# Splitting half of the scan's operator evictions between VectorE and ScalarE, with a new order of the scan's stages and of the end, in a bidirectional RWKV-7 layer

## The chip, the cores and the metric

The kernel runs on one core of a Trainium2 chip. The metric is the device time of one execution in microseconds; the time of before is the median of three runs. A core has TensorE (PE; its weight loads are listed as PEld), VectorE (DVE), ScalarE (ACT), GpSimd (POOL) and SyncE (SP, which issues the DMAs here). Each works through its own list of instructions in order; they meet at semaphores.

## The reference

The layer mixes 128 context tokens and 2048 latent tokens of width 1024. Half of the width goes through RWKV-7 heads (8 of 64 channels), in both directions; the other half is a short gated convolution. What matters here is the recurrence of a head:

```python
def step(S, inp):                    # S: 64x64 state of each head and direction
    r_t, w_t, k_t, v_t, kk_t, a_t = inp
    s_kk = jnp.einsum('bdhij,bdhj->bdhi', S, kk_t)
    S = (S * w_t[..., None, :] - s_kk[..., :, None] * (kk_t * a_t)[..., None, :]
         + v_t[..., :, None] * k_t[..., None, :])
    return S, jnp.einsum('bdhij,bdhj->bdhi', S, r_t)
s_final, ys = lax.scan(step, s0, xs)
y = ys[:, 0] + jnp.flip(ys[:, 1], axis=1)     # then a norm per head, a bonus term, a gate
...
u = concat([ya, yb]) @ w_out
return x + gate * u, s_final                  # and a final RMS norm of x
```

The context starts from zero states and returns its final ones; the latent tokens start from cached states.

## The kernel before

Phase 1 (to about 950 us) makes the projections, the convolution and the scan's inputs. Phase 2 is the scan, phase 3 the output projection with the final norm.

**The scan in stages.** A sequential recurrence is turned into matmuls over chunks of 64 tokens. There are 17 stages, 0 to 16; stage 15 is the context. A stage takes, for each direction (0 and 1), eight units; a unit is one chunk of a pair of heads. Its work is cut into words, and the last digit of a word is the direction:

- `L` loads the inputs of a direction (`rr`), `fs`, `gs` and `sv` further ones (tiles `stf`, `stg`/`sth`, `sv`); all are DMAs of SP.
- `Gm`, `Qm`, `Fm` are products on PE into PSUM; `Ge`, `Fe` (DVE, with a mask, L1037) and `Qe`, `Fa` (ACT, copies) bring them to SBUF. `F` is split so: ACT copies columns 0 to 63, DVE masks columns 64 to 127.
- `dg`, `ab` (DVE, L1058 and L1063) gather 32x32 blocks, `zi` (ACT) writes an identity, `pre` (DVE, L1081 and L1082) multiplies and subtracts once, and `I` inverts the blocks on POOL: 45 instructions a stage, 15 multiplications (L1091) and 30 subtractions (L1094). `I` waits for `pre` of its stage.
- `zr`, `zd` (DVE transposes, L1102 and L1105), `c0`, `c1` (ACT), `U` (PE), `bu` (ACT), `W` (PE), `n` (ACT, L1130) join the blocks to 64x64 inverses, in this order. `X` solves on PE; `Xc` (ACT, L1175) copies the result to `stf`.
- `E` makes the operators: eight words a stage, `Eijd` with d the direction, each 16 matmuls (L1189) into one PSUM tile of 128x512; `Ev` brings it to SBUF on DVE with a mask (L1194).
- `S` (PE, L1220) and `sv` (DVE, L1246) are the recurrence itself: eight state steps a direction, each of which needs the `sv` before it. `y` collects outputs; for the context `sv` writes `so`, which goes to DRAM as a final state.
- `fw`, `fr`, `fq`, `fm`, `T`, `fy`, `fa` finish a block of outputs.

**The order.** The string SEQ is one body: the words in the order in which each engine gets them, where `X+k` is word X of stage b+k in body b. PE, DVE and ACT keep this order in bodies 0 to 12 (FIXED = 13); ahead of these a scheduler places the words, and it places POOL's and SP's instructions everywhere. From body 13 to the end the string LATE is the order, where `X@s` is word X of stage s. It also holds phase 3's words: `WL`, `WH`, `WD` load and split the output weight (`woh`, `wol`), `AL`, `AH`, `AD` and `CL`, `CH`, `CD` load and split the inputs (`mhc`, `mlc`), `AP0@t`, `AP1@t` are the twelve matmuls each (tile `psa`) of the convolution's half of the inputs of token tile t with either half of the output's columns, which need no output of the scan, and `R`, `Lo` change pools.

**PSUM.** IN_PM lists the words whose tiles come from the pool `pm`; `T`, `U`, `W` and `S` share `pS`, the rest `p2`. A product in PSUM waits for a free buffer of its pool, which comes back when its eviction is done.

Of the kernel before, what the change touches and what calls it, by code (L numbers as in the profile page):

```python
# [10 lines left out]
ALU = mybir.AluOpType  # L11
# [741 lines left out]


SEQ = """
S00 sv51+-1 fa+-1 S61+-1 Ge0+3 dg0+3 gh10+1 sv61+-1 E110 sv00 S71+-1 svL1+1 y10+-1 Ev001 S10 c1+1 Ev110 sv10
E111 sv71+-1 Ev111 E010 E101 y11+-1 E011 gsL1+2 fsL1+1 bu+1 Ev010 I+2 S20 Ev101 fw Ev011 sv20 S01 E100
fsL0+1 gsL0+2 sv01 fr Ev100 Gm1+3 Ge1+3 dg1+3 W+1 S11 Qm1+3 gh11+1 gh00+1 ab+3 fq Fm0+3 S30 n+1 Qe1+3 Qm0+3
L0+4 sv11 Fa0+3 Qe0+3 zi+3 sv30 S40 Fe0+3 fm S21 sv40 sv21 Fm1+3 L1+4 X0+1 S50 pre+3 T sv50 Fa1+3 Fe1+3 S31
S60 sv31 Xc00+1 init+1 y00 Xc10+1 X1+1 S41 Xc01+1 sv60 S70 svL0+2 zr+2 sv41 E000+1 sv70 fy Xc11+1 Ev000+1  # L760
zd+2 S51 gh01+2 U+2 y01 Gm0+4 E001+1 c0+2
"""
IN_PM = "E001 E011 E101 E110 Fm1 Gm1 Qm0 Qm1 X1".split()
IN_S = "T U W".split()
FIXED = 13
LATE = """
I@15 sv51@12 fa@10.1 Ge0@16 E110@13 Ev001@13 gh10@14 E010@13 Ev110@13 E100@13 gh00@14 Ev010@13 Gm1@16
fsL0@14 Ev100@13 gh11@14 S00@13 Ge1@16 S61@12 E111@13 c1@14 sv00@13 E011@13 sv61@12 bu@14 dg0@16 S10@13
Ev011@13 S71@12 E101@13 svL1@14 fw@11.0 sv10@13 sv71@12 y10@12 S20@13 fsL1@14 Ev111@13 S01@13 y11@12 W@14
sv20@13 sv01@13 Ev101@13 S30@13 n@14 S11@13 sv30@13 sv11@13 S40@13 fr@11.0 X0@14 sv40@13 fq@11.0 dg1@16  # L770
X1@14 fm@11.0 Xc00@14 ab@16 S50@13 S21@13 Xc10@14 T@11.0 Xc01@14 E000@14 sv50@13 sv21@13 S60@13 Ev000@14
E010@14 zi@16 Xc11@14 sv60@13 S31@13 Ev010@14 S70@13 E100@14 svL0@15 sv70@13 sv31@13 pre@16 I@16 E110@14 Ev100@14
fy@11.0 E001@14 fsL0@15 gsL0@15 gh00@15 Ev110@14 S00@14 Fm1@16 gh10@15 sv00@14 fa@11.0 S10@14 E011@14
fw@11.1 Fa1@16 y01@13 sv10@14 y10@13 Ev011@14 S41@13 S20@14 y00@13 sv41@13 E111@14 sv20@14 Ev001@14
S51@13 S30@14 sv51@13 E101@14 sv30@14 zr@15 S61@13 fsL1@15 gsL1@15 gh01@15 S40@14 sv40@14 U@15 sv61@13 zd@15
gh11@15 S50@14 fr@11.1 S71@13 svL1@15 c0@15 sv50@14 sv71@13 S60@14 Ev111@14 c1@15 sv60@14 Ev101@14 S70@14
svL0@16 sv70@14 Fm0@16 bu@15 Fe1@16 y10@14 Qm1@16 Fa0@16 S01@14 fq@11.1 W@15 sv01@14 Qe1@16 Fe0@16 S11@14
fm@11.1 n@15 Qm0@16 sv11@14 Qe0@16 X0@15 R@0 CL@5 CL@4 S21@14 Xc00@15 T@11.1 sv21@14 S31@14 fy@11.1 Xc10@15
sv31@14 fa@11.1 y11@13 X1@15 y00@14 S41@14 Xc01@15 sv41@14 y01@14 S51@14 Xc11@15 sv51@14 S61@14 sv61@14
S71@14 CH@4 E110@15 svL1@16 sv71@14 E100@15 CH@5 CD@4 fw@14.0 CD@5 WL@0 zr@16 WL@1 zd@16 U@16 fr@14.0 c1@16  # L780
y11@14 c0@16 Ev100@15 Ev110@15 E111@15 bu@16 E101@15 Ev111@15 WH@0 E000@15 Ev101@15 WH@1 E001@15 WD@0
Ev000@15 fq@14.0 E011@15 fm@14.0 W@16 fsL1@16 gsL1@16 gh01@16 Ev001@15 WD@1 CL@7 Ev011@15 E010@15 gh11@16
T@14.0 fsL0@16 gsL0@16 gh10@16 S00@15 CL@6 fy@14.0 S30@15 S20@15 S01@15 gh00@16 S11@15 fa@14.0 S31@15 S21@15
sv30@15 n@16 Ev010@15 sv00@15 sv20@15 fw@14.1 X1@16 CH@7 fr@14.1 S10@15 S40@15 S60@15 Xc01@16 CD@7 S70@15
Xc11@16 sv40@15 WL@3 sv11@15 sv01@15 sv21@15 sv10@15 CH@6 X0@16 S50@15 CD@6 Xc00@16 S41@15 S61@15 S51@15
sv51@15 Xc10@16 WL@2 sv50@15 sv41@15 sv70@15 sv31@15 fq@14.1 E110@16 fm@14.1 E000@16 sv60@15 WH@3 sv61@15
S71@15 Ev110@16 sv71@15 E111@16 WD@3 Ev000@16 E001@16 Ev111@16 E101@16 Ev001@16 WH@2 AL@5 E100@16 y10@15
WD@2 Ev100@16 y00@15 T@14.1 E010@16 fy@14.1 S00@16 fa@14.1 S01@16 Ev010@16 AH@5 E011@16 AD@5 AL@6 Lo@0 xL@5
sv00@16 AP0@5 y01@15 y11@15 aL@5 fc@15.1 AP1@5 AE0@5 Ev101@16 fw@15.1 fr@15.1 xL@6 sv01@16 Ev011@16 AH@6
S10@16 S11@16 AE1@5 AD@6 aH@5 sv10@16 AP0@6 AL@7 fq@15.1 aD@5 fm@15.1 aL@6 sv11@16 AP1@6 AE0@6 P0l@5 B0@5  # L790
AH@7 AE1@6 AD@7 aH@6 cL@8 aD@6 aL@7 AP0@7 Z0@5 G0@5 AP1@7 AE0@7 P1l@5 B1@5 AE1@7 cH@8 cD@8 cL@9 P0l@6 B0@6
# [24 lines left out]
def phase2(K):
    nc, tc, A, S = K.nc, K.tc, K.A, K.S
    V, G, P, T = nc.vector, nc.gpsimd, nc.scalar, nc.tensor
    D = nc.sync.dma_start
    MF, MG, ME = (0, 1), (0, 1), (2, 3)  # L820
    B = Ctx()
# [151 lines left out]
    def stage(s):  # L973

        if s in sts:
            return sts[s]
        st = sts[s] = Ctx()
        st.g = []
        st.fin = None
        for d, units, blk in stages[s]:  # L980
            g = Ctx()
            g.d, g.units, g.blk = d, units, blk
            g.E, g.ps, g.sp = {}, {}, {}
            st.g.append(g)
        return st

# [190 lines left out]
    def operator(name, s, st, gi):  # L1177

        g = st.g[gi]
        n, h2 = (int(c) for c in name[-3:-1])  # L1180
        us = half(g, n)
        k = (h2 if g.d == 0 else 1 - h2) * 2
        if name[:2] != "Ev":
            lt, rt = (g.fs, g.gs) if g.d == 0 else (g.gs, g.fs)
            pe = g.ps[name] = psum(name, s, [128, 2, 2, 128])
            for i in range(2):
                for hd in range(2):
                    for b, r in enumerate((H0, H1)):
                        T.matmul(pe[r, i, hd, :].rearrange("p (b t) -> p b t", b=2), lt[:, b, hd, us.start + k + i], rt[:, :, hd, us.start + k + i], start=True, stop=True)  # L1189
# [4 lines left out]
        V.tensor_tensor(g.E[n][:, k:k + 2].rearrange("p a b c -> p (a b) c"), pe[:].rearrange("p a b c -> p (a b) c"),  # L1194
                        B.msk[:, ME[g.d]].unsqueeze(1).broadcast_to((128, 4, 128)), ALU.mult)
# [137 lines left out]
    def ending(name, s, st, gi):  # L1333
# [3 lines left out]
        if st.fin is not None:  # L1337
# [311 lines left out]
```

## Time and profile before

| | us |
|---|---|
| median of 3 runs | 1579.01 (1577.63 to 1589.78) |
| profiled execution | 1579.98 |
| its span, first to last instruction | 1578.2 |
| busy: PE, DVE, ACT, POOL | 1496.3, 1138.5, 772.6, 574.6 |
| granted TensorE clock, mean | 0.989 |
| inverses of stages 2 to 16 on POOL, first start to last end | 963.21 to 1331.81 |

The shares of busy time are averages over three phases; the page's row of POOL in 40 slices stands at 8 tenths in the scan and at 0 to 3 elsewhere. The answers used below are of five kinds: the waits of an engine (total, times, longest), its timeline (start, length, engine, line, operation, out<-in, shape, how many instructions are joined; in brackets the idle time before, and who ended it), groups by line and shape (how many, then busy time and mean ns, then idle time before), busy time by window, and transfers by tile.

### The profile page before, as it was taken

The numbers are of one execution on the slowest core, as the hardware profiler recorded it, in microseconds if no ns is written. First come the engines' busy times: TensorE is split into PE (matmuls) and PEld (weight loads), VectorE is DVE, ScalarE is ACT, GpSimd is POOL, SyncE is SP. The second block draws the span as 40 slices with busy tenths as digits, with TensorE's granted clock in tenths as the row PEclk, the third lists the DMA queues.
The fourth block names the chain that finished last, engine by engine and source line by source line (L and its number), as shares of the span: only waits on it lengthen the run. The fifth ranks groups of instructions, "written<-read, shape, count | busy, mean of one in ns | idle before, by whom it ended". The sixth has DMA issues, their size and how long they took to land.

```text
span 1578.2 us, 39386 instructions
## 1 busy us (share of the span) xinstructions
PE 1496.3 (95%) x16208; PEld 1377.9 (87%) x16208; DVE 1138.5 (72%) x1957; ACT 772.6 (49%) x1462; POOL 574.6 (36%) x962
## 2 busy tenths in 40 slices
PE   5899989999999999999999998999999997799998
PEld 2899989999999999899999997887888786678786
DVE  5999995673999735449995437899898987646533
ACT  4566652432555313225651107887878777523222
POOL 0133320000333100013322805888888887212221
PEclk9999999999999999999999998999999999999999
DMA  9669998663877875447887536566675754645442
GB/s 370 211 186 264 265 266 324 214 217 118 214 228 228 200 241 182 142 140 205 257 252 267 196 124 170 163 185 174 192 202 163 192 157 149 183 139 189 149 143 93
DMA packets 204580, 313.78 MB, mean 199 GB/s; under 512 B 58089, under 2 KB 147561, under 8 KB 190321
## 3 DMA queue, kind: packets, MB, share of 16 engines
q1 hardware_dynamic: 168816, 311.13, 63.6%
q10 hardware_dynamic: 35584, 0.14, 1.4%
q8 instruction: 127, 2.08, 0.6%
q14 instruction: 53, 0.43, 0.1%
HBM read 208.05 MB, written 103.17 MB: 197 GB/s over the span
## 4 chain that ended last, share of the span: by engine, by line
PE 61%; DVE 18%; DMA 8%; issue 5%; POOL 4%; ACT 3%; SPq 1%; ACTq 0%; DVEq 0%; POOLq 0%
PE psu L1503 4%; PE psu L1504 4%; PE psu L1505 4%; PE psE L1189 3%; POOL zt L1094 3%; PE mmb L182 2%; PE mmb L184 2%; PE mmb L183 2%; PE psS L1220 2%; PE mmc L182 2%; PE mmc L184 2%; PE mmc L183 2%; PE mmu L184 2%; PE mmgb L184 2%; PE mmu L182 2%
## 5 line engine op out<-in xcount | busy, mean ns | idle before, releaser
L1094 POOL TENSOR_TENSOR zt<-zt,ztmp 128x30 f32<-128x30 f32 (+7 forms) x510 | 217.6, 427 | 39.8
L1091 POOL TENSOR_TENSOR ztmp<-ab,zt 128x60 f32<-128x60 f32 (+7 forms) x255 | 138.2, 542 | 63.7 <-DVE ab L1082 44.0
L410 POOL TENSOR_TENSOR sh<-rawl 128x384 f32<-128x384 f32 (+1 forms) x48 | 46.9, 994 | 209.9 <-ACT rawl L401 209.9
L1220 PEld LDWEIGHTS psS<-sv,E 128*64 128x64 f32 x2176 | 81.3, 138 | 40.3 <-DVE sv L1246 18.8
L1220 PE MATMUL psS<-sv,E 128*64 128x64 f32 x2176 | 102.2, 229 | 14.8 <-DVE sv L1246 11.0
L1194 DVE TENSOR_TENSOR E<-psE,msk 128x512 f32<-128x512 f32 x136 | 90.6, 683 | 16.6 <-PE psE L1189 15.4
L1568 POOL TENSOR_TENSOR z<-z,x 128x512 f32<-128x512 f32 x32 | 42.7, 1338 | 146.5 <-DVE z L1562 86.0
L1175 ACT ACTIVATE stf<-psX 64x512 f32<-64x512 f32 x136 | 80.3, 591 | 11.2 <-PE psX L1171 8.8
L434 POOL TENSOR_TENSOR hsl<-sq,hsh 128x384 fp32r<-128x384 f32 (+1 forms) x24 | 34.0, 1417 | 130.6 <-ACT hsh L429 130.6
L1246 DVE TENSOR_TENSOR sv<-psS,pc 64x128 f32<-64x128 f32 x254 | 62.7, 273 | 22.5 <-PE psS L1220 21.8
L182 PE MATMUL mmg<-h,w 128*128 128x384 f32 (+1 forms) x216 | 70.8, 328 | 0.0
L183 PE MATMUL mmg<-h,w 128*128 128x384 f32 (+1 forms) x216 | 70.7, 327 | 0.0
L184 PE MATMUL mmg<-h,w 128*128 128x384 f32 (+1 forms) x216 | 70.6, 327 | 0.0
L219 POOL TENSOR_TENSOR hslq<-ssq,hshq 128x384 fp32r<-128x384 f32 (+1 forms) x4 | 4.8, 1208 | 176.9 <-ACT hshq L218 176.9
L182 PE MATMUL mmb<-h,w 128*128 128x384 f32 (+1 forms) x192 | 63.6, 331 | 5.8 <-DMA w<-scr_wsp 3.3
L184 PE MATMUL mmc<-h,w 128*128 128x384 f32 (+1 forms) x192 | 63.5, 331 | 0.9 <-DVE w L154 0.9
L182 PE MATMUL mmv<-h,w 128*128 128x384 f32 (+1 forms) x192 | 63.0, 328 | 1.0 <-DVE sg L524 0.9
L182 PE MATMUL mmc<-h,w 128*128 128x384 f32 (+1 forms) x192 | 63.6, 331 | 0.0
L184 PE MATMUL mmb<-h,w 128*128 128x384 f32 (+1 forms) x192 | 63.5, 331 | 0.0
L183 PE MATMUL mmc<-h,w 128*128 128x384 f32 (+1 forms) x192 | 63.3, 330 | 0.0
L183 PE MATMUL mmb<-h,w 128*128 128x384 f32 (+1 forms) x192 | 63.3, 330 | 0.0
L184 PE MATMUL mmu<-h,w 128*128 128x384 f32 (+1 forms) x192 | 62.8, 327 | 0.0
(312 smaller groups left out, 5009.8 us busy)
## 6 DMA issues: line engine op xcount, KB each, us to landing
w<-scr_wsp SPq DMA_DIRECT2D x68, 1024.0 KB, 6.8
scr_wsp<-w SPq DMA_DIRECT2D x34, 1024.0 KB, 6.1
rr<-scr_ops SPq DMA_DIRECT2D x32, 1024.0 KB, 6.2
scr_ops<-xs SPq DMA_DIRECT2D x160, 192.0 KB, 6.1
wr<-in_win SPq DMA_DIRECT2D x34, 512.0 KB, 6.8
x<-in_x SPq DMA_DIRECT2D x17, 512.0 KB, 3.7
wadas<-in_wada SPq DMA_DIRECT2D x8, 1024.0 KB, 13.7
sv<-scr_vt SPq DMA_DIRECT2D x32, 256.0 KB, 3.8
```

Of the source, the lines that this page charges most:

```text
L182: T.matmul(ps[:, :n], w[:, 0, k], hh[:, 0, k, :n], start=k == 0, stop=False)
L183: T.matmul(ps[:, :n], w[:, 0, k], hh[:, 1, k, :n], start=False, stop=False)
L184: T.matmul(ps[:, :n], w[:, 1, k], hh[:, 0, k, :n], start=False, stop=k == 7)
L1091: G.tensor_tensor(tv, ab[:, j:j + 2, j + 2:32].unsqueeze(1).broadcast_to((128, kn, 2, n)), zt[:, :kn, j:j + 2].unsqueeze(3).broadcast_to(( ...
L1094: G.tensor_tensor(zt[:, :kn, j + 2:32], zt[:, :kn, j + 2:32], tv[:, :, r], ALU.subtract)
L1175: P.activation(g.fs[64:128, :, hd, e::2], g.ps["X"][e][hr_].rearrange("p a (b t) -> p b a t", b=2), AF.Copy, scale=-1.0)
L1194: V.tensor_tensor(g.E[n][:, k:k + 2].rearrange("p a b c -> p (a b) c"), pe[:].rearrange("p a b c -> p (a b) c"), B.msk[:, ME[g.d]].unsquee ...
L1220: T.matmul(g.sp[i // 4][r, q, hd, :], g.E[n][:, k, hd, r], g.sv[:, u, hd, :], start=True, stop=True)
L1246: V.tensor_tensor(dst, g.sp[i // 4][0:64, q], B.pc[0:64, d, 2 * p:2 * p + 2, c:c + 1].broadcast_to((64, 2, 64)), ALU.mult)
L1503: T.matmul(ps[:], mh[:, n], hi[:, cs], start=start and n == 0, stop=False)
L1504: T.matmul(ps[:], mh[:, n], lo[:, cs], start=False, stop=False)
L1505: T.matmul(ps[:], ml[:, n], hi[:, cs], start=False, stop=stop and n == 3)
```

## The change

A new word `Ea` lets ACT copy columns 0 to 63 of an operator, for four of the eight words of a stage (E000, E001, E100, E101). No mask applies to these columns. `Ev` of such a word then covers columns 64 to 127 alone; it follows `Ea` in the list and waits for it. All three order strings are new.

```diff
+        dst, pe = (x.rearrange("p a b c -> p (a b) c") for x in (g.E[n][:, k:k + 2], g.ps["E" + name[-3:]][:]))
+        if name[:2] == "Ea":
+            P.copy(dst[:, :, 0:64], pe[:, :, 0:64])
+            g.plain.add(name[-3:])
+            return
+        c0 = 64 if name[-3:] in g.plain else 0
+        V.tensor_tensor(dst[:, :, c0:], pe[:, :, c0:], B.msk[:, ME[g.d], c0:].unsqueeze(1).broadcast_to((128, 4, 128 - c0)), ALU.mult)
+        g.ps.pop("E" + name[-3:])
...
-IN_PM = "E001 E011 E101 E110 Fm1 Gm1 Qm0 Qm1 X1".split()
+IN_PM = "E011 Fm0 Fm1 Gm0 Gm1 X1".split()
...
-fsL0+1 gsL0+2 sv01 fr Ev100 Gm1+3 Ge1+3 dg1+3 W+1 S11 Qm1+3 gh11+1 gh00+1 ab+3 fq Fm0+3 S30 n+1 Qe1+3 Qm0+3
+fq U+1 Qm0+3 Qe1+3 sv20 S21 Ge1+3 dg1+3 ab+3 fm S30 sv21 Fm0+3 E110 L0+4 gh00+1 Ev110 bu+1 W+1
```

In SEQ the loads are spread: `L0+4` stands at 0.48 of the list and `L1+4` at 0.77 (0.54 and 0.66 before), the `fs` loads at 0.60 and 0.64 (0.35 and 0.25), the `gs` loads at 0.59 and 0.89 (0.24 and 0.36). The first operator of the next stage stands 0.27 of the list behind its `fs` load, `Gm0+4` 0.51 behind `L0+4`. `U` of a stage moves from the end of one body to 0.36 of the next. In LATE, `Gm` to `pre` of stage 16 come near the beginning, and `AP0@5`, `AP1@5`, `AP0@6` stand between the words of stages 15 and 16.

Below, the first number behind `psF`, `psX` or `psE` is the stage, the two behind `psS` are the direction and the first step of a half (0 or 4), the rest number buffers; shapes are partitions x elements. Lines of `phase2` have moved by one, and from the operators on by six (L1194 is now L1200, L1246 is L1252, L1306 is L1312).

The first place is DVE in a full body (stage 6's operators, stage 9's products), from `ab` to the first instruction of `pre`. Before:

```order
L1063 STREAM_TRANSPOSE ab_13008<-dg_12786 128x32x32
L1246 TENSOR_TENSOR sv_12319<-psS_1_0_12921,pc 64x128
L1246 TENSOR_TENSOR sv_12194<-psS_0_0_12772,pc 64x128
L1037 TENSOR_TENSOR F_8365<-psFm_9_1356_13011,msk 128x4x64
L1037 TENSOR_TENSOR F_8365<-psFm_9_1357_13012,msk 128x4x64
L1305 RECIPROCAL yss_12938<-yss_12938 128x8
L1306 TENSOR_TENSOR y_10261<-y_10261,yss_12938 128x512
L1246 TENSOR_TENSOR sv_12194<-psS_0_4_13051,pc 64x128
L1246 TENSOR_TENSOR sv_12319<-psS_1_0_12921,pc 64x128
L1081 TENSOR_TENSOR dg_12786<-ab_13008 128x512
```

Now:

```order
L1064 STREAM_TRANSPOSE ab_12985<-dg_12884 128x32x32
L1311 RECIPROCAL yss_12898<-yss_12898 128x8
L1312 TENSOR_TENSOR y_10363<-y_10363,yss_12898 128x512
L1252 TENSOR_TENSOR sv_12315<-psS_1_0_12878,pc 64x128
L1200 TENSOR_TENSOR E_1339_12807<-psE_6_1357_13014,msk 128x512
L1038 TENSOR_TENSOR F_8365<-psFm_9_1355_12996,msk 128x4x64
L1038 TENSOR_TENSOR F_8365<-psFm_9_1356_12997,msk 128x4x64
L1252 TENSOR_TENSOR sv_12254<-psS_0_0_12764,pc 64x128
L1200 TENSOR_TENSOR E_1346_12896<-psE_6_1360_13074,msk 128x512
L1082 TENSOR_TENSOR dg_12884<-ab_12985 128x512
```

Two whole operator evictions have moved in between `ab` and `pre`, and two of the four state steps there have moved out.

The second place is ACT in the same body, from the last copies of a solve to the merge of the stage after it. Now:

```order
L1176 ACTIVATE stf_9577<-psX_6_1325_12667 64x2x4x64 x2
L1196 COPY E_1330_12735<-psE_6_1329_12726 128x4x64
L1273 COPY y_12771<-psS_1_0_12388 64x512
L1161 COPY stg_9583<-GA_8369 64x8x64
L1162 COPY stg_9583<-Q_8370 64x8x64
L1112 COPY zb<-zd_12695 32x16x32 x2
L1196 COPY E_1337_12799<-psE_6_1336_12786 128x4x64
L1196 COPY E_1339_12807<-psE_6_1335_12775 128x4x64
L1273 COPY y_12771<-psS_1_4_12697 64x512
L1273 COPY y_12646<-psS_0_4_12650 64x512
```

The rows of L1196 are new, here three of the stage's four; the others were there before, in another order.

The third place is PE near the end, at stage 16's solve and operators. Before, from the last rows of the operators on:

```order
L1317 MATMUL psT_1743_17473<-idt_8359,y_16671 128x2x64 x4
L1189 MATMUL psE_16_1744_17478<-stg_9582,stf_9576 64x128 x8
L1220 MATMUL psS_0_0_17489<-sv_16807,E_1736_17430 64x64 x4
L1220 MATMUL psS_1_0_17497<-sv_17018,E_1740_17452 64x64 x4
L1189 MATMUL psE_16_1745_17506<-stf_9577,stg_9583 64x128 x8
L1503 MATMUL psa_0_17536<-woh_16928,mhc_17503 128x512
```

Now, from the end of the solve to the first operators and the third product:

```order
L1172 MATMUL psX_16_1727_17444<-F_8374,zb 64x128 x2
L1226 MATMUL psS_0_4_17282<-sv_16761,E_1710_17218 64x64 x4
L1226 MATMUL psS_0_4_17282<-sv_16761,E_1702_17136 64x64 x4
L1226 MATMUL psS_1_4_17477<-sv_16724,E_1705_17176 64x64 x8
L1226 MATMUL psS_1_4_17477<-sv_16724,E_1707_17196 64x64 x8
L1190 MATMUL psE_16_1734_17512<-stf_9577,stg_9583 64x128 x8
L1190 MATMUL psE_16_1735_17525<-stg_9582,stf_9576 64x128 x8
L1509 MATMUL psa_0_17540<-woh_16707,mhc_17440 128x512
```

The first matmul of `psa` stood behind the last operator; now one `psa` group stands ahead of each half of the solve, one behind the first two operators, and state steps of stage 15 (`psS_0_4`, `psS_1_4`) lie ahead of these.

More of the change, by code (lines that the diff above doesn't have):

```diff
@@ L772 @@
[L772 to L791, printed above, removed]
@@ new lines @@
+S21@15 AP1@5 Xc10@16 fa@14.0 sv21@15 y01@15 sv70@15 AH@6 X1@16 AD@6 S60@15 Xc01@16 S50@15 WL@3 sv60@15
+S41@15 S51@15 sv50@15 S71@15 sv41@15 S61@15 sv51@15 Xc11@16 sv71@15 sv61@15 y10@15 E001@16 WH@2 y11@15
+E100@16 fc@15.1 Ea001@16 WD@2 AP0@6 Ea100@16 AE1@5 Ev001@16 Ev100@16 WH@3 AL@7 E111@16 AE0@6 WD@3 fw@15.1
+E010@16 Ev111@16 E110@16 Ev010@16 E000@16 Ev110@16 fr@15.1 E101@16 Ea000@16 Ev000@16 Ea101@16 E011@16
+fq@15.1 Ev101@16 AP1@6 Lo@0 Ev011@16 aL@5 xL@5 fm@15.1 AH@7 S01@16 T@15.1 sv01@16 AE1@6 AD@7 S11@16 S00@16
@@ new lines @@
+sv11@16 AP0@7 cL@8 sv00@16 xL@6 aH@5 fy@15.1 aD@5 fa@15.1 aL@6 AP1@7 AE0@7 P0l@5 S21@16 AE1@7 B0@5 sv21@16
+cH@8 aH@6 cD@8 aD@6 aL@7 cL@9 S31@16 S10@16 sv31@16 P1l@5 B1@5 y01@16 sv10@16 Z0@5 G0@5 S41@16 aH@7 S20@16
+sv41@16 P0r@6 B0@6 sv20@16 aD@7 Q0@5 Z1@5 aL@8 G1@5 S51@16 S30@16 sv51@16 P1r@6 sv30@16 S61@16 y00@16 S40@16
+xL@7 Q1@5 B1@6 sv61@16 sv40@16 Z0@6 ss@5 G0@6 aH@8 S71@16 S50@16 sv71@16 P0l@7 rt@5 B0@7 y11@16 sv50@16
+fw@16.1 aD@8 Q0@6 fr@16.1 aL@9 Z1@6 fq@16.1 S60@16 P1l@7 B1@7 sv60@16 G1@6 fm@16.1 rc@5 fo@5 xL@8 S70@16
```

82 lines of the change are left out of this document (45 added, 37 removed).

## The prediction

> **What bounds the kernel now.** I read the window table first, because the span mixes three phases. Its columns are window, length, then busy time and instruction count of PE, PEld, DVE, ACT and POOL, then the granted clock.
>
> ```profile
> 963.21:1331.81 368.60, 341.54 (x8756) 300.07 (x8750) 322.25 (x654) 291.93 (x552) 315.98 (x684) 1.00 0.63 175
> 1125.00:1149.50 24.50, 23.08 (x597) 20.17 (x593) 24.01 (x50) 18.51 (x36) 21.05 (x45) 1.00 0.70 198
> 1331.80:1372.30 40.50, 29.88 (x601) 25.80 (x597) 27.36 (x51) 24.23 (x38) 12.18 (x6) 0.94 0.56 164
> 1372.30:1389.00 16.70, 15.52 (x80) 11.85 (x78) 7.72 (x15) 4.67 (x10) 0.10 (x1) 1.00 0.75 236
> 1389.00:1570.60 181.60, 181.60 (x864) 145.62 (x862) 89.19 (x148) 48.09 (x118) 42.73 (x32) 1.00 0.44 142
> ```
>
> The first row holds 15 inverses of the scan, the second one stage out of it, where DVE is busy 24.01 of 24.50 us. By that row DVE looks like the bound, and the change takes work from DVE. The waits of POOL say otherwise:
>
> ```profile
> POOL ztmp L1091 <- DVE ab L1082: 14.5, 1, 14.5
> ```
>
> This is every wait that POOL has in 963 to 1331.8 us (total, times, longest), and it is the one with which the window begins. The timeline of POOL shows a seam between two inverses:
>
> ```profile
> 963.21 0.29 POOL L1091 TENSOR_TENSOR ztmp<-ab,zt 128x60 f32<-128x60 f32 x1 [14.51 <-DVE ab L1082]
> ...
> 1157.68 0.60 POOL L1094 TENSOR_TENSOR zt<-zt,ztmp 128x30 f32<-128x30 f32 x2
> 1158.36 0.29 POOL L1091 TENSOR_TENSOR ztmp<-ab,zt 128x60 f32<-128x60 f32 x1
> ...
> 1307.15 0.63 POOL L1215 MEMSET sv<- 64x128 f32 x4
> ...
> 1331.21 0.60 POOL L1094 TENSOR_TENSOR zt<-zt,ztmp 128x30 f32<-128x30 f32 x2
> ```
>
> An inverse ends at 1158.28, the next begins at 1158.36. From 963.21 to 1331.81 they follow each other so: 368.60/15 = 24.57 us each. POOL's busy sum (315.98) hides this, since it leaves out the short pauses between its 684 instructions. Who follows whom is seen on DVE:
>
> ```profile
> 1155.51 0.69 DVE L1082 TENSOR_TENSOR ab<-ab,dg 128x512 f32<-128x512 f32 x1
> 1158.31 1.08 DVE L1102 STREAM_TRANSPOSE zr<-zt 128x512 f32<-128x512 f32 x1
> 1182.74 1.08 DVE L1102 STREAM_TRANSPOSE zr<-zt 128x512 f32<-128x512 f32 x1 [1.32 <-POOL zt L1094]
> ```
>
> DVE ends the preparation (`pre`) of the next inverse at 1156.20, 2.16 us before POOL takes it up, and starts `zr` at 1158.31, 0.03 us after the inverse's end; for the next `zr`, at 1182.74, it idles 1.32 us. So **POOL bounds the scan** and DVE keeps 2 to 3 us in hand. From 1331.81 PE bounds: in the last window it is busy for 181.60 of 181.60 us, and ahead of that it idles 40.50 − 29.88 + 16.70 − 15.52 = **11.8 us**. Only these 11.8 us, the seams and the start can be won without a faster POOL.
>
> **The change, part by part.**
>
> *The split eviction.* The two engines' prices are in the window's groups:
>
> ```profile
> L1194 DVE TENSOR_TENSOR E<-psE,msk 128x512 f32<-128x512 f32 x120 | 79.9, 683 | 12.0 <-PE psE L1189 10.9
> L1037 DVE TENSOR_TENSOR F<-psFm,msk 128x256 f32<-128x256 f32 x58 | 21.5, 411 | 0.7 <-ACT F L1051 0.7
> L1051 ACT COPY F<-psFm 128x256 f32<-128x256 f32 x58 | 18.9, 376 | 9.8 <-PE psFm L1019 9.8
> ```
>
> Eight evictions (120/15) belong to a stage. Four of them go from 128x512 (683 ns) to 128x256, and `F` is that size: 4 × (683 − 411) = 1.09 us less on DVE a stage; four copies like `F`'s come to ACT, 4 × 376 = 1.50 us. ACT goes from 18.5 to 20 of 24.5 us. Value on the path: **0**, since POOL covers both; if POOL were no cover it would be −1.1 us a stage (a rival below).
>
> Does it lengthen or shorten POOL's inverse? DVE work stretches POOL's instructions only in some cases. POOL's timeline beside DVE's:
>
> ```profile
> 1129.99 1.40 POOL L1091 TENSOR_TENSOR ztmp<-ab,zt 128x112 f32<-128x112 f32 x1
> 1134.63 0.38 POOL L1091 TENSOR_TENSOR ztmp<-ab,zt 128x112 f32<-128x112 f32 x1
> 1130.01 1.11 DVE L1081 TENSOR_TENSOR dg<-ab 128x512 f32<-128x512 f32 x1
> ...
> 1145.05 0.99 POOL L1094 TENSOR_TENSOR zt<-zt,ztmp 128x128 f32<-128x128 f32 x2
> 1120.29 0.99 POOL L1094 TENSOR_TENSOR zt<-zt,ztmp 128x128 f32<-128x128 f32 x2
> 1144.71 1.89 DVE L1194 TENSOR_TENSOR E<-psE,msk 128x512 f32<-128x512 f32 x3
> ```
>
> The same multiplication takes 1.40 us under `pre` and 0.38 without it; the pair of subtractions takes 0.99 under three operator evictions and 0.99 elsewhere. Halving these evictions gives POOL **0**.
>
> The two halves of an operator lie in one PSUM tile, as those of `F` do, and there DVE waits for ACT:
>
> ```profile
> DVE F L1037 <- ACT F L1051: 0.7, 1, 0.7
> ```
>
> So a split operator is ready 376 + 411 = 787 ns after its product at the earliest, against 683 now, and DVE, which works in order, stands at its half until ACT has come to the copy. [...]
>
> *The start* (the first inverse of the steady part begins at 963.21). Both `Gm` products of stage 2 now share one PSUM pool; PE still has its transposes and products of other stages around them. Bounds −0.4 and +0.5, taken **+0.1**.
>
> *The first ordered body.* There the preparation is just in time:
>
> ```profile
> 981.61 2.13 DVE L1063 STREAM_TRANSPOSE ab<-dg 128x1024 f32<-128x1024 f32 x1
> ...
> 986.30 0.69 DVE L1082 TENSOR_TENSOR ab<-ab,dg 128x512 f32<-128x512 f32 x1
> ```
>
> It ends at 987.00 and the inverse before it at 987.12. The new list puts two full evictions between `ab` and `pre`: 2 × 0.68 − 0.12 = 1.25 us late if `ab` stays where it is, 0 if the work taken out ahead of `ab` moves it up, and 2 if the evictions wait for PE as well. I take **+1.0**. In later bodies the same two evictions eat 1.4 of the 2.2 us in hand, while 1.1 us comes back from the smaller ones: **0**.
>
> *The moved loads.* SP's transfers, from issue to landing:
>
> ```profile
> rr<-scr_ops SPq DMA_DIRECT2D x25, 1024.0 KB, 5.6
> stf<-scr_ops SPq DMA_DIRECT2D x28, 256.0 KB, 5.0
> ```
>
> The closest user after the move is the first operator of a direction-0 stage, 0.27 of the list behind its `fs` load, 6.6 of 24.6 us against 5.0; `Gm` stands 0.5 of the list, 12 us, behind its `L`, against 5.6. They stay hidden: **0**. If `fs` landed 3 us later, 1.4 us of wait would begin on PE, inside the 2 to 3 us in hand.
>
> *The last seam.* Four small memsets of the context's states (from 1307.15) delay the last inverse, which starts at 1307.76; four more and a copy of a held state (0.28) interrupt it later. In the new order `pre` of stage 16 comes early, and POOL has all eight memsets inside the last inverse and the copy behind it. The memsets cost their 1.26 us there as before: **−0.3** (−0.6 if they find POOL idle, +0.5 if one waits for its buffer).
>
> *The end.* PE's largest idle times after the last inverse:
>
> ```profile
> PE psE L1189 <- DVE E L1194: 6.4, 5, 3.8
> PE psX L1171 <- ACT stf L1175: 1.4, 2, 0.8
> PE psU L1119 <- DVE zr L1102: 1.0, 1, 1.0
> ...
> 1362.94 0.28 DVE L1246 TENSOR_TENSOR so<-psS,pc 64x128 f32<-64x128 f32 x1 [3.96 <-DMA out_nst<-so]
> 1372.27 0.50 PE L1503 MATMUL psa<-woh,mhc 128*128 128x512 f32 x1
> 1377.66 0.39 PE L1505 MATMUL psa<-woh,mlc 128*128 128x512 f32 x1
> 1388.53 0.50 PE L1503 MATMUL psa<-woh,mhc 128*128 128x512 f32 x1 [1.18 <-ACT mhc L1490]
> ```
>
> The longest, 3.8 us, is an operator's product that waits for an eviction, which stands on DVE behind `so`, and that waits for the transfer of an earlier state. The new list gives PE work for such times: AP0@5 and AP1@5 are the 24 matmuls from 1372.27 to 1378.05, 5.8 us or 2.9 each, and with AP0@6 8.7 us are placed between stage 16's merges, solves and operators. It also leaves more of PE's work behind the last inverse: two operators of stage 15 (0.9) and four state steps of stage 14 (4 × 0.46), 2.8 us. Without any idle, therefore, the end gains 11.8 − 2.8 = 9.0; with all of it left, it loses 2.8. I walked the new order after the last inverse by these durations. Before, stage 16's operators end 40.5 us after it, and with the 8.7 of AP and the 1.2 of idle at 1388.53 this is 50.4. In the new order the same work is 29.9 + 2.8 + 8.7 = 41.4, and I find 3.5 us of idle (the merge `U` waits for `zr`, `W` for the copies of the merge, and one solve for its copies), since products that need no scan stand next to each longer wait: 44.9. Value **−5.5**. What is late next is the chain `zr`, `U`, `W`, `X` itself, and from 1389 on PE's own work.
>
> The sum goes against the profiled execution, 1579.98 us (1.8 beside its span), 0.97 above the median of the runs, 1579.01: 1579.98 + 0.1 + 1.0 − 0.3 − 5.5 = **1575.3**.
>
> **The rivals.**
>
> *The end stays as it is.* The new fillers need `mhc` tiles from ACT, whose list at the end gets stage 16's copies too; if these are late, PE waits at AP instead. Then 1579.98 + 0.1 + 1.0 − 0.3 = 1580.8, and up to 2.8 more: about 1582. For it: the wait for `mhc` at 1388.53. Against it: at 40.5 us ACT is busy for 24.2 only. It is inside the range.
>
> *DVE bounds the full stages.* Then 1.1 us comes off each of the 13 ordered bodies, and the sum is 1575.3 − 14.2 = 1561. For it: 24.01 of 24.50. Against it: DVE's idle before `zr`, and POOL's lack of any wait.
>
> *Slower: DVE waits for ACT.* DVE's half eviction has `ab` and `pre` behind it, and ACT has its copy behind others that wait in their turn:
>
> ```profile
> ACT zb L1130 <- PE psW L1127: 21.4, 15, 4.6
> ```
>
> That is 1.4 us a stage. If each of the four copies finds ACT held up that long, DVE stands 4 × 1.4 = 5.7 us at its halves; it has 2.6 us in hand and 1.1 from the smaller evictions, so 2.0 a body reach POOL: 13 × 2.0 = 26, about 1601. It decides from 3.7/4 = 0.93 us a copy; at half the delay nothing is seen. For it: the wait is new, and sits ahead of `pre`. Against it: in ACT's new order the copies stand behind those of `stf`, `zb` and `y`, and none directly behind the wait for `W`.
>
> *The change does not do as it says*: the operators come later than before, so that state steps wait though DVE is freed. That is the mechanism just named at a smaller size, 0 to +10: 1575 to 1585.
>
> **How the numbers follow.** Forecast with its bounds, 0.70: the low end is 1579.98 − 0.4 + 0 − 0.6 − 9.0 = 1570, the high end 1579.98 + 0.5 + 2.0 + 0.5 + 2.8 = 1586; it takes in the rival with the unchanged end. DVE as the bound: 0.11. Slower by DVE's waits for ACT: 0.13. Late operators past 1586: 0.06. The range goes from **1566 to 1588**; below it remains most of DVE as bound (about 0.09), above it most of the slower rival (0.11). One per cent, 15.8 us, is about what a measurement of this kernel can tell from no change. Faster by more, under 1563.2: 0.09. Slower by more, over 1594.8: 0.09. Within: 0.82.
>
> **What the profile after would show.** POOL's inverses follow each other with 0.08 us from about 963 on, with one seam near 987 of up to 2 us; an inverse still takes 24.6 us. If DVE waits for ACT, its row of waits for `E` from ACT is over 3.7 us a stage, and POOL has a wait for `ab` L1083 in many bodies. On DVE the evictions fall into two groups of 64, and ACT has 68 copies of `E` near 376 ns. After the last inverse PE's idle up to the steady end is about 6 us instead of 11.8, the first `psa` stands before stage 16's solve, and no wait of 3.8 us remains on PE for `E`. The prediction is wrong if POOL waits for `pre` in the ordered bodies, if an inverse's own time changes from 24.6 us, or if the last window is not full on PE.

## The result: slower by 0.8 per cent, and the profile after

The changed kernel takes 1596.60 us (median of 20 runs) against 1582.04 for the one before (20 runs): a ratio of 1.0083, 95% interval 1.007 to 1.0096. The forecast was 1575.3, with a range that ended at 1588. The profiled execution took 1594.97 us, its span 1593.0, 14.8 more than the span before.

First the waits of POOL, again from the start of the steady scan to the last inverse (total, times, longest):

```profile
POOL ztmp L1092 <- DVE ab L1083: 44.7, 10, 15.2
```

Before, there was one wait, of 14.5 us, with which the window began. Now there are nine more, 29.5 us in all. POOL's timeline gives the two marks that I use below, the starts of inverse 3 and of inverse 13 (first the changed kernel's, then the one before's):

```profile
988.86 0.29 POOL L1092 TENSOR_TENSOR ztmp<-ab,zt 128x60 f32<-128x60 f32 x1 [5.34 <-DVE ab L1083]
1246.50 0.29 POOL L1092 TENSOR_TENSOR ztmp<-ab,zt 128x60 f32<-128x60 f32 x1 [3.95 <-DVE ab L1083]
```

```profile
987.20 0.28 POOL L1091 TENSOR_TENSOR ztmp<-ab,zt 128x60 f32<-128x60 f32 x1
1232.79 0.29 POOL L1091 TENSOR_TENSOR ztmp<-ab,zt 128x60 f32<-128x60 f32 x1
```

Ten stages took 257.6 us instead of 245.6. The whole difference of the spans splits so:

| | before | after | difference |
|---|---|---|---|
| to the start of inverse 3 | 987.20 | 988.86 | +1.7 |
| inverse 3 to inverse 13 | 245.59 | 257.64 | +12.0 |
| inverse 13 to the end of the last | 99.02 | 100.93 | +1.9 |
| from there to the end of the span | 246.39 | 245.57 | −0.8 |

So the loss sits in the full bodies of the scan, where the forecast had 0. TensorE's ledger names its kind. The windows after (length, busy time of PE, PEld, DVE, ACT, POOL, PEclk, DMA share, GB/s) are the scan, the 57 us behind it, and the rest:

```profile
960.92:1347.43 386.51, 348.26 (x8676) 306.36 (x8676) 308.71 (x644) 307.68 (x605) 305.02 (x683) 0.97 0.63 165
1347.43:1404.60 57.17, 51.92 (x818) 43.50 (x817) 36.66 (x79) 37.51 (x67) 12.45 (x7) 0.94 0.64 181
1404.60:1585.50 180.90, 179.86 (x868) 145.28 (x866) 86.62 (x144) 48.48 (x118) 43.09 (x32) 1.00 0.45 147
```

The scan is 17.9 us longer (386.51 against 368.60). PE idles 38.25 of it instead of 27.06, 11.2 more, and is busy for 348.26 instead of 341.54, 6.7 more although 80 fewer matmuls fall into it, at a granted clock of 0.97 instead of 1.00. DVE is busy for 13.5 us less: the smaller evictions are there. What PE's new idle time waits for is in its waits, first after, then before:

```profile
PE psS L1226 <- DVE sv L1252: 11.8, 22, 2.8
PE psGm L1020 <- issue: 7.2, 3, 2.6
PE psE L1190 <- issue: 6.9, 7, 2.1
PE psS L1226 <- issue: 4.4, 3, 1.8
```

```profile
PE psS L1220 <- DVE sv L1246: 11.0, 30, 1.3
PE psE L1189 <- issue: 4.0, 4, 1.5
...
PE psFm L1019 <- issue: 1.3, 1, 1.3
PE psU L1119 <- issue: 1.3, 2, 0.8
PE psGm L1019 <- issue: 0.7, 1, 0.7
...
PE psS L1220 <- issue: 0.4, 2, 0.2
...
PE psX L1171 <- issue: 0.4, 1, 0.4
```

"issue" is time in which PE waits for no semaphore that the profile shows. It grew from 8.1 to 18.5 us: 10.4 of the 11.2. The longest of these waits, in PE's timeline:

```profile
1095.92 0.97 PE L1020 MATMUL psGm<-rr 64*64 64x128 f32 x25
1099.49 0.70 PE L1020 MATMUL psGm<-rr 64*64 64x128 f32 x7 [2.60 <-issue]
```

PE stops in the middle of 32 like matmuls, whose inputs are all there. What happens then on the DMA side is in SP's timeline (the changed kernel, then the one before, a body each):

```profile
1084.60 0.37 SPq L1010 DMA_DIRECT2D rr<-scr_ops  x1
1085.58 0.58 SPq L957 DMA_DIRECT2D stf<-scr_ops  x1
1086.22 2.09 SPq L957 DMA_DIRECT2D stg<-scr_ops  x2
1088.36 0.60 SPq L957 DMA_DIRECT2D stf<-scr_ops  x1
1089.40 0.38 SPq L1010 DMA_DIRECT2D rr<-scr_ops  x1
```

```profile
1070.50 0.58 SPq L956 DMA_DIRECT2D stg<-scr_ops  x1
1071.13 1.77 SPq L956 DMA_DIRECT2D stf<-scr_ops  x2
1072.95 0.61 SPq L956 DMA_DIRECT2D stg<-scr_ops  x1
1073.65 1.13 SPq L1286 DMA_DIRECT2D w<-scr_q  x1
1077.45 2.50 SPq L1009 DMA_DIRECT2D rr<-scr_ops  x2
```

Before, the four small loads (1 MB) begin at 1070.50 and the two big ones (2 MB) 7 us later. Now all six, 3 MB, are issued within 5 us. The list spreads them, but SP's order is the scheduler's, and SP stands at the first `rr` until `Fm`'s matmuls have read the tile (68.2 us in 18 such waits from 963 to 1290 us); behind it everything is free to go. The DMA view of 1089.3 to 1096.7 us (queue, packets, MB, share of the 16 engines) has one queue:

```profile
q1 hardware_dynamic: 972, 1.85, 106.0%
```

In 7.4 us no packet of an instruction queue started. In the next 1.8 us one did in each of the two such queues (16 and 8 KB), and PE went on:

```profile
q1 hardware_dynamic: 546, 0.43, 100.6%
q8 instruction: 1, 0.02, 3.9%
q14 instruction: 1, 0.01, 1.2%
```

My reading, **theory F**: TensorE's instructions come by DMA, the fetch waits behind the burst, PE runs dry. The trace does not show this as such; the times of its DMA packets fit the first and the last part: all nine of PE's issue waits of 1 us or more in the scan end 1.3 to 1.6 us after a 16 KB packet of q8 has landed. And q8's packets go with TensorE's instructions, about 250 to a packet: 68 for 17,352 matmuls and weight loads in the scan, 7 for 1,734 in the last window. Whether the packets come late because of the loads is what the experiments below test.

PE's clock follows:

```profile
1089.20:1096.80 7.60, 7.39 (x190) 6.37 (x181) 6.72 (x17) 6.92 (x14) 6.35 (x17) 1.00 1.06 254
1098.80:1105.60 6.80, 6.11 (x71) 5.78 (x73) 2.38 (x7) 1.64 (x4) 5.94 (x12) 0.50 0.20 61
1105.60:1112.40 6.80, 6.80 (x192) 6.05 (x192) 5.52 (x12) 6.11 (x12) 5.78 (x14) 1.00 0.28 80
```

From 1098.80 us on, 0.7 us before the idle time of 2.6 us ends, the granted clock is 0.50 for 6.8 us, with 71 matmuls where the next 6.8 us have 192. Four such stretches at 0.50, of 3.4 or 6.8 us, begin in the changed kernel's scan, each within 1.5 us of the end of an idle time of 1.8 to 2.8 us. Not every idle time of this size has one: issue waits of 2.1, 1.8 and 2.2 us, which end at 994.3, 1177.6 and 1305.4 us, had no half clock behind them. Nor does every half belong to the burst: of the four, two go with issue waits (3.4 us at 0.50 with a wait of 2.4, 6.8 with the one of 2.6), one with a wait for ACT of 1.8 and one with a wait for DVE of 2.8 (3.4 us each). What decides between these cases is not shown.

The rivals: **theory A**, that DVE waits for ACT's copies (my own rival in the prediction), and **theory O**, that the new order of the words is itself longer than POOL's 24.6 us.

### The profile page after: what moved, and what is told of

It is laid out like the page before. It is cut to its first block, busy times and chain, and to the rows that moved or that the text cites. A ratio compares the mean times of both kernels' runs of the same rounds, so it can differ in the third digit from the quotient of the medians.

```text
span 1593.0 us, 39522 instructions
## 1 busy us (share of the span) xinstructions
PE 1504.3 (94%) x16208; PEld 1385.8 (87%) x16208; DVE 1124.4 (71%) x1957; ACT 794.9 (50%) x1530; POOL 561.7 (35%) x962
## 3 DMA queue, kind: packets, MB, share of 16 engines
q8 instruction: 127, 2.08, 0.6%
## 4 chain that ended last, share of the span: by engine, by line
PE 74%; DVE 11%; DMA 5%; issue 4%; ACT 3%; SPq 1%; ACTq 0%; POOL 0%; DVEq 0%; POOLq 0%
PE psE L1190 7%; PE psS L1226 4%; PE psu L1509 3%; PE psu L1511 3%; PE psu L1510 3%; PE psGm L1020 2%; PE psFm L1020 2%; PE mmb L182 2%; PE mmb L184 2%; PE mmc L182 2%; PE mmb L183 2%; PE mmc L184 2%; PE mmc L183 2%; PE mmu L184 2%; PE mmu L182 2%
## 5 line engine op out<-in xcount | busy, mean ns | idle before, releaser
L1095 POOL TENSOR_TENSOR zt<-zt,ztmp 128x30 f32<-128x30 f32 (+7 forms) x510 | 208.1, 408 | 39.9
L1226 PE MATMUL psS<-sv,E 128*64 128x64 f32 x2176 | 106.4, 230 | 19.5 <-DVE sv L1252 13.1
L1226 PEld LDWEIGHTS psS<-sv,E 128*64 128x64 f32 x2176 | 87.9, 140 | 40.8 <-issue 18.9
L1252 DVE TENSOR_TENSOR sv<-psS,pc 64x128 f32<-64x128 f32 x254 | 64.7, 274 | 52.2 <-PE psS L1226 50.8
L1200 DVE TENSOR_TENSOR E<-psE,msk 128x512 f32<-128x512 f32 (+1 forms) x136 | 74.1, 548 | 25.7 <-PE psE L1190 12.7
L182 PE MATMUL mmb<-h,w 128*128 128x384 f32 (+1 forms) x192 | 62.9, 328 | 3.4 <-DMA w<-scr_wsp 1.7
L184 PE MATMUL mmc<-h,w 128*128 128x384 f32 (+1 forms) x192 | 62.8, 327 | 1.1 <-DVE w L154 1.1
L182 PE MATMUL mmc<-h,w 128*128 128x384 f32 (+1 forms) x192 | 63.1, 329 | 0.0
L184 PE MATMUL mmu<-h,w 128*128 128x384 f32 (+1 forms) x192 | 62.8, 327 | 0.0
L184 PE MATMUL mmk<-h,w 128*128 128x384 f32 (+1 forms) x184 | 60.3, 328 | 2.6 <-DVE w L154 2.6
L184 PE MATMUL mmb<-h,w 128*128 128x384 f32 (+1 forms) x192 | 62.8, 327 | 0.0
L182 PE MATMUL mmu<-h,w 128*128 128x384 f32 (+1 forms) x192 | 62.7, 327 | 0.0
## 6 DMA issues: line engine op xcount, KB each, us to landing
wadas<-in_wada SPq DMA_DIRECT2D x8, 1024.0 KB, 13.8
```

The costliest lines, as they stand in the source:

```text
L182: T.matmul(ps[:, :n], w[:, 0, k], hh[:, 0, k, :n], start=k == 0, stop=False)
L184: T.matmul(ps[:, :n], w[:, 1, k], hh[:, 0, k, :n], start=False, stop=k == 7)
L1095: G.tensor_tensor(zt[:, :kn, j + 2:32], zt[:, :kn, j + 2:32], tv[:, :, r], ALU.subtract)
L1200: V.tensor_tensor(dst[:, :, c0:], pe[:, :, c0:], B.msk[:, ME[g.d], c0:].unsqueeze(1).broadcast_to((128, 4, 128 - c0)), ALU.mult)
L1226: T.matmul(g.sp[i // 4][r, q, hd, :], g.E[n][:, k, hd, r], g.sv[:, u, hd, :], start=True, stop=True)
L1252: V.tensor_tensor(dst, g.sp[i // 4][0:64, q], B.pc[0:64, d, 2 * p:2 * p + 2, c:c + 1].broadcast_to((64, 2, 64)), ALU.mult)
```

## The experiments

The sizes below are ratios to the kernel before on the same chip, with 95% intervals. "Ten stages" is the time from the start of inverse 3 to that of inverse 13, read as above: 245.6 before, 257.6 after.

**Whole evictions with the new lists.**

```diff
-Ev001 ... Ea001 ... (all Ea words of both lists)
+Ev001 ...           (every Ev whole)
```

> The changed kernel with its new lists, but every operator evicted whole on VectorE (128x512), no copies on ScalarE. Theory F: TensorE's own instruction fetch waits behind a burst of six loads (3 MB in 4 to 5 us, rr, stf, stg, stg, stf, rr), TensorE then idles 1 to 2.6 us and its granted clock halves; the split has no part in it. F expects the time of the changed kernel, 1592 to 1600, with TensorE's idle put down to issue in the scan still 15 us or more. Theory A: VectorE waits for ScalarE's copies (9.8 us in the scan), so without them the scan returns to VectorQueue lengths of before: 1578 to 1585. Theory O: the new order itself is longer than GpSimd's 24.6 us a body even without either: 1590 to 1605, more than the changed kernel by about 1 us a body since VectorE has 1.1 us more to do.

1600.34 us, ratio 1.0111 (1.0059 to 1.0163); ten stages 261.1. Theory A falls as the cause here: without any copy on ACT the loss stays. The interval overlaps the changed kernel's, so what the split is worth in the new lists stays open. DVE's waits in the changed kernel's scan agree; this is the row, 0.7 us a stage where my rival asked for 3.7:

```profile
DVE E L1200 <- ACT E L1196: 9.8, 19, 2.9
```

**The split alone, in the old lists.**

```diff
-... Ev001 ... Ev101 ... Ev100 ... Ev000+1
+... Ea001 Ev001 ... Ea101 Ev101 ... Ea100 Ev100 ... Ea000+1 Ev000+1
```

> The kernel before, with its own lists, and the four ScalarE copies put into them right ahead of the VectorE halves they belong to. Theory F: no change of the loads, so 1577 to 1583, GpSimd's inverses still without a wait. Theory A: VectorE waits for ScalarE, 4 times a body, and GpSimd for VectorE: 1588 to 1600.

1588.48 us, ratio 1.0063 (1.0038 to 1.0088): above F's range, at the low end of A's. Ten stages took 246.7, so POOL kept its pace there. But DVE does wait for ACT in this kernel, 39.2 us:

```profile
DVE E L1199 <- ACT E L1195: 39.2, 39, 6.9
```

So A's wait exists in the old lists. In the full bodies it fits into what DVE had in hand; in the first ordered body it does not (29.0 us from inverse 2 to inverse 3 instead of 24.0, with 8.2 us of waits for ACT on DVE there); behind inverse 13 the scan took 101.1 us instead of 99.0 and the end 249.9 instead of 246.4. F alone does not explain this kernel, and it does not carry the burst.

**The loads apart, in the new lists.** Three kernels keep SP to the list's order and put the second `rr` load elsewhere: at the list's end, at 0.83 of it, and (SP kept in bodies 0 to 12 alone) at 0.88.

```diff
-engines={PE, DVE, Activation}
+engines={PE, DVE, Activation, SP}
-... X1+1 L1+4 Xc01+1 ... Ev000+1 svL0+2 Gm0+4
+... X1+1 Xc01+1 ... Ev000+1 svL0+2 Gm0+4 L1+4
```

> The changed kernel with SyncE kept to the list's order, and L1+4 moved from 0.77 of the body's list to its end, so that the two 1 MB loads stand half a body apart and the six loads no longer follow each other within 5 us. Theory F: TensorE's idle put down to issue in the scan falls from 18 us to under 8, no half clock in the scan, GpSimd waits under 10 us after its first inverse, time 1574 to 1582. Theory A and theory O: nothing of it changes, 1592 to 1600.

1593.22 us, ratio 1.0081 (1.0056 to 1.0105). The ten stages fell to 247.5 us, and "issue" in the scan to 4.3, as F has it. The whole did not follow: the 100.9 us behind inverse 13 became 104.5, and the end 249.4 instead of 245.6. There, too, SP was kept to a list that was made for another order, and PE waited for the loads' data (the rows are of the whole scan; all four waits of over 2 us stand behind inverse 13):

```profile
PE psQm L1029 <- DMA rr<-scr_ops: 8.1, 6, 2.6
PE psE L1190 <- DMA stf<-scr_ops: 4.8, 5, 2.1
```

> The changed kernel with SyncE kept to the list's order and L1+4 behind zd+2 (0.83 of the list, between its place in the change, 0.77, and the end, where TensorE waited 13 us for rr and stf). Theory F: issue idle under 8 us, waits for rr and stf under 5 us, scan 370 to 376, whole 1575 to 1584. Theory O: scan 380 or more as with the load at the end.

1592.59 us, ratio 1.0073 (1.0042 to 1.0103); ten stages 248.0, then 103.0 and 251.2: the same picture in the times. But "issue" in the scan is 13.4 us, not under 8 as expected, and the ten stages are short all the same, so the sum of "issue" alone does not give the loss.

> The changed kernel with SyncE kept to the list's order in bodies 0 to 12 alone (from body 13 on its order is the scheduler's again, as in the change) and L1+4 behind gsL0+2, at 0.88 of the list. Two kernels with the loads apart took 247.5 and 248.0 us from the start of inverse 3 to that of inverse 13, where the changed one took 257.6 and the one before 245.6, but lost it again behind body 13, where SyncE was kept to the list too. Theory F: 246 to 249 us for these ten inverses and the changed kernel's 101 and 246 behind them or a little less, whole 1577 to 1585. If the order behind body 13 was not the reason, 1588 to 1594 again.

1590.80 us, ratio 1.0063 (1.0037 to 1.0090); ten stages 250.7, then 104.3 and 245.1. The end came back, as expected, but not the stages behind inverse 13, and the whole lies in the range that I had given for the case that SP's order behind body 12 was not the reason. The bodies were less good: all six loads followed each other again, within 6.4 us in the body at 1111 us ("issue" 13 us in the scan). So placing the loads alone takes back most of the ten stages' 12 us, but none of these three is a kernel to keep.

**Fewer bytes.** The new lists with every instruction of the compute engines, but `rr` loads of a quarter of the size in stages 4 to 14, and the kernel before with the same as its control.

```diff
-D(g.rr[:, 0:4] ..., src ...)                  # 1 MB
+D(g.rr[:, 0:4, 0:m] ..., src[:, :, :m * 64])  # m = 2 of 8 units
```

> The changed kernel, in which stages 4 to 14 load only 2 of 8 units of rr (256 KB instead of 1 MB, twice a stage) and take stage 3's inputs instead of their own, so its output is not the layer's; every instruction of the compute engines is there as before. Theory F (TensorE's instruction fetch waits behind the loads, its clock halves after the idle time): TensorE's idle put down to issue in the scan falls from 18 us to under 5, GpSimd's inverses from body 4 on without waits, the scan 368 to 374 us instead of 386.5, the whole 1572 to 1582. Theory O (the new order is itself too long for GpSimd's 24.6 us): scan 380 or more, whole 1588 or more.

1581.20 us, ratio 0.9991 (0.9971 to 1.0011). Ten stages took 243.7 us. POOL has one wait beside the first, and PE's waits in the scan have no row of "issue" at all; these are all that it has:

```profile
POOL ztmp L1096 <- DVE ab L1087: 20.5, 2, 15.1
...
PE psS L1230 <- DVE sv L1257: 23.8, 40, 3.1
PE psE L1194 <- DVE E L1204: 1.2, 2, 0.7
PE psGm L1024 <- ACT stf L1180: 1.0, 1, 1.0
PE psE L1194 <- ACT stf L1180: 0.6, 1, 0.6
PE psGm L1024 <- DMA rr<-scr_ops: 0.2, 1, 0.2
PE psX L1176 <- ACT zb L1135: 0.2, 1, 0.2
```

Theory O falls: the same order of the same instructions on PE, DVE and ACT runs at POOL's pace once the burst is small.

> The kernel before with the same reduced loads and the same exchange of inputs in stages 4 to 14 (its output is not the layer's): the control. GpSimd bounds its scan, so fewer bytes change nothing by either theory: scan 366 to 370 us, whole 1575 to 1582. If it falls below 1572, the loads cost the kernel before too.

1579.57 us, ratio 0.9998 (0.9977 to 1.0019), ten stages 245.9: the loads cost the kernel before nothing.

**The burst in the kernel before.** Its own order and whole evictions, but the four small loads moved behind `L0+4` and SP kept to that.

```diff
-gsL1+2 fsL1+1 ... fsL0+1 gsL0+2 ... L0+4 ... L1+4
+L0+4 fsL0+1 gsL0+2 gsL1+2 fsL1+1 ... L1+4
```

> The kernel before with whole evictions and its own order on TensorE, VectorE and ScalarE, but the fs and gs loads moved right behind L0+4 and SyncE kept to that order, so that the six loads of a body follow each other as in the changed kernel. Theory F: TensorE's idle put down to issue grows from 7 us to 15 or more in the scan, GpSimd gets waits, time 1588 to 1600. Theories A and O: same as before, 1577 to 1583.

1620.85 us, ratio 1.0256 (1.0218 to 1.0293), above F's range; ten stages 278.8. Part of that is that `stf` itself lands too late in this order, so it does not separate the fetch from the data:

```profile
PE psE L1190 <- DMA stf<-scr_ops: 19.7, 19, 3.5
PE psE L1190 <- issue: 9.5, 6, 2.0
...
PE psU L1120 <- issue: 7.3, 2, 3.7
```

**A load that nobody waits for.** This separates them: the kernel before, with SP kept to its list in bodies 0 to 12 and one more transfer of 1 MB in stages 4 to 14, from DRAM into a DRAM scratch that nothing reads.

```diff
 D(g.rr[:, 0:4] ..., src ...)
+if gi == 1 and 4 <= s <= 14:
+    D(S["dum"].rearrange("k p t -> p k t"), src.rearrange("k p t -> p k t"))
```

> The kernel before, SyncE kept to its list in bodies 0 to 12, and a third load of 1 MB behind the two rr loads of stages 4 to 14, from DRAM into a DRAM scratch that nothing reads or waits for. Theory F: TensorE's instruction fetch waits behind it, so issue idle in the scan goes from 7 us to 20 or more, half clocks appear, and GpSimd waits: 1590 to 1610. If TensorE only suffers where a load that it needs is late, nothing changes: 1577 to 1583, or it shows as waits for rr, stf and stg.

1593.02 us, ratio 1.0073 (1.0052 to 1.0094); ten stages 258.3. PE's waits in the scan have no row for a DMA; "issue" adds up to 27.0 us, of which the first rows are

```profile
PE psE L1191 <- issue: 7.8, 6, 3.0
PE psU L1121 <- issue: 6.0, 5, 1.7
...
PE psS L1222 <- issue: 4.4, 4, 2.6
PE psGm L1021 <- issue: 4.0, 3, 1.6
```

> The control of the one with the third load: the kernel before with SyncE kept to its list in bodies 0 to 12 and nothing else. Its list has the same loads in the same two groups as the scheduler made, so 1577 to 1583, issue idle about 7 us in the scan.

The control, with SP kept to the list and no third load: 1585.20 us, ratio 1.0028 (1.0007 to 1.0049), a little over what I expected, ten stages 249.9. Its "issue" is 15.1 us, twice what I expected; why keeping SP to the list does that is open. Against it the transfer alone makes 7.8 us by the medians, and 8.4 us in ten stages and 12 us of "issue" by the profiles. The profiles overstate it: the one with the transfer is of its longest execution (1599.63 us), the control's of its shortest (1581.98). In the kernel with the transfer eleven of twelve issue waits of 1 us or more end 1.3 to 1.6 us after a 16 KB packet has landed.

**The new end behind the old scan.** The list of before up to body 12, the changed kernel's end behind it.

```diff
 SEQ = (that of before)
-LATE = I@15 gh01@13 fa@10.0 ... E001@13 ... Ea001@13 ...
+LATE = I@15 sv51@12 fa@10.1 S61@12 Ev001@13 E010@13 ... Ev010@13 ... gh11@14 ...
```

> The scan's list of before (whole evictions, its loads) up to body 12, and from body 13 the changed kernel's end with its split evictions and early products. If the forecast for the end was right (-5.5 us) and only the scan's loads spoiled it, this gives 1570 to 1576, with TensorE idling about 6 us in the 57 us after the last inverse instead of 11.8. If the end gains nothing, 1578 to 1584.

1579.29 us, ratio 0.9990 (0.9972 to 1.0008): no gain. PE's idle time behind the last inverse did fall, to 57.30 − 52.12 = 5.2 us from 11.8, and was given back, to more work behind the last inverse (1684 matmuls from there to the end instead of 1540) and to the clock:

```profile
1329.70:1387.00 57.30, 52.12 (x812) 43.74 (x811) 37.64 (x78) 36.72 (x65) 13.35 (x15) 0.88 0.62 168
1330.30:1344.00 13.70, 12.17 (x190) 10.43 (x192) 8.67 (x16) 9.33 (x15) 3.64 (x6) 0.50 0.64 168
```

For 13.7 us PE ran at 0.50, and the end took 247.2 us against 246.4. Why the clock stays at 0.50 so long here, and in the kernel before for 3.4 us at a time (from 1330.0 and from 1364.1 us), is not settled: it is one execution each.

> The scan's list of before up to body 12 and the changed kernel's end from body 13 on, as in the kernel that came to 0.999 of the time before, but with every eviction whole on VectorE. If ScalarE's copies hold up the end's other copies, this is the faster one, 1572 to 1577, and the only version under the time before; if the copies help the end, or if the early products are eaten by half clocks behind the last inverse, 1578 to 1582.

1582.85 us, ratio 1.0014 (0.9998 to 1.0030). Not faster either, so ScalarE's copies of operators are not what holds up the end; idle behind the last inverse 57.20 − 49.55 = 7.7 us in the same window, the clock 0.88 there again. No version that I ran beats the kernel before.

## Why the prediction was wrong

**The step that failed is "the moved loads: they stay hidden: 0".** I compared the distance in the list between a load and its first user with its landing time, and that part held: PE hardly waits for `stf` or `rr` in the changed kernel's scan (once for a load of `stf`, 0.8 us). But I took SP's order from the list, though SP's instructions are not kept to it, and did not ask what else uses the DMA queues. What came in place of the 0 is +12.0 us in ten stages, of the 19.5 us by which the span missed the forecast. By theory F six loads in a row hold up TensorE's instruction packets, and that is a wait without a releaser in the profile: 10.4 us more of it in the scan, with 6.7 us more of busy time on top, part of it slow clock (0.97 in the mean of the scan instead of 1.00). That the bytes of the loads do it is shown, since with a quarter of `rr` both the waits and the 12 us were gone; that the packets queue behind the loads is inferred from that. Its sign was in the profile before: waits for "issue" of up to 1.5 us, and on the page a queue of the kind instruction, with 127 packets and 2.08 MB, 16 KB each.

**What bounds the kernel** was right, and the conclusion from it too wide. POOL did bound the scan, by the control with fewer bytes as well. But "DVE keeps 2 to 3 us in hand" is only an answer to small delays: PE, busy for 341.5 of 368.6 us, has little to catch up with, and a body that loses more passes it on to POOL through `ab` and `pre`, in waits of 0.8 to 5.3 us.

**The split eviction** gained nothing in the full bodies, as forecast, and cost little there: alone, in the old lists, it took ten stages from 245.6 to 246.7 us. Outside them it was not free, since that kernel is 0.6 per cent longer. The copies took 374 ns against 376. That halved evictions leave POOL alone cannot be read from the changed kernel's inverses, which take 22.4 to 25.9 us where POOL waits between them. With small `rr` loads POOL ran without waits from body to body: 24.4 us a stage with the split, 24.6 in the control without it, so the split did not lengthen an inverse.

**The first ordered body**: +1.1 with the start by forecast, +1.7 measured at the start of inverse 3; that these are close is luck. In this pair inverse 2 began 2.3 us earlier, and `ab` at the same time as before. But inverse 2 to inverse 3 took 27.9 us instead of 24.0, and so it is in the other runs: 27.4 to 28.4 us in all six kernels with the new lists, 24.0 to 25.1 in the seven with the old body and whole evictions. The start of inverse 2 varies between runs (958.6 to 964.6 us) and does not explain it: at 964.3 us the new lists took 28.0, at 964.6 the old one 25.1. So the term of +1.0 is nearer +3 to +4, by one execution of each kernel. ACT's copies are not the reason (28.1 us without them); what is stays open.

**The last seam**: +1.9 between inverse 13 and the last end instead of −0.3, with one more wait for `ab`, 2.0 us, in it.

**The end**: −5.5 by forecast, −0.8 measured. Both terms were off. From the last inverse to the end PE is busy for 231.8 us instead of 227.0, 4.8 more where I had 2.8: 1684 matmuls stand there instead of 1540, and my two operators and four state steps are only 64 of these 144. And it idles for 13.8 us instead of 19.4, 5.6 less where the sum has 8.3 (11.8 to 3.5); in the 57 us behind the inverse 57.17 − 51.92 = 5.3 us are left. The "about 6" in my list of signs fits this, but not my sum. Where the scan ran on time, in the kernel with small `rr` loads, the end took 240.8 us (1612 matmuls), 5.6 less than before and 4.2 less than in its control; it is near the forecast's number, but of one execution with fewer bytes.

**The rival "slower: DVE waits for ACT"** named the right side, the right place of arrival (`pre` late, POOL waiting) and the wrong cause: 9.8 us of such waits in the whole scan. That its 1601 us lies near the measured 1596.60 is luck. The range left out the mechanism that came.

## What to carry to other kernels

Read the order of every queue that the change moves, the DMA-issuing one too, from what was built and not from the list that asks for it: here SP stood 68.2 us at `rr` loads whose tile was still being read, and once one could go, all six loads of a body were issued within 5 us. Look for idle time put down to issue, and compare it with bursts of megabytes: here PE stopped for 2.6 us behind 3 MB of loads, and 1 MB more a stage that nothing reads went with 12 us more of such waits in the scan (27.0 against 15.1). Where PE is nearly full (busy for 341.5 of 368.6 us here), such a stop can cost more than itself: with the one of 2.6 us came 6.8 us at a granted clock of 0.50, though behind three others of 1.8 to 2.2 us it stayed at 1.00.

## What was not expected of the hardware

A transfer that nothing reads or waits for slowed a kernel by 0.5 per cent against its control (1593.02 us against 1585.20), most likely through TensorE's instruction supply. That the 16 KB packets are TensorE's is inferred, since the profile names no engine for them: their number goes with its instructions, about 250 to a packet, and its issue waits end 1.3 to 1.6 us after one has landed. And with idle times of 1.8 to 2.8 us the granted clock was 0.50 for 3.4 or 6.8 us in four places of the changed kernel's scan, and stayed at 1.00 behind three others of 1.8 to 2.2 us; why is open.
